# Masks written by VectorE instead of added by matmuls, and squares summed by TensorE, in a 16-head mixer and a stick-breaking layer

## The chip, the core and the metric

The program runs on one core of a Trainium2 chip. The metric is the device time of one execution in microseconds (us), the median over several runs. Engines are called PE (TensorE, with PEld for its weight loads), DVE (VectorE), ACT (ScalarE), POOL (GpSimd) and SP (SyncE, which issues most transfers).

## The reference

The input is one sequence of 256 tokens of width 1024, in float32. A first block with a mixer and a feed-forward part is followed by a second one with two layers: retention, and stick-breaking attention, each between feed-forward parts. What matters here are the two places with a mask and one with a sum of squares.

```python
# first block: differential attention (8 heads, two score maps each) and latent attention (8 heads)
def chunk_causal_attention(q, k, v, scale):
    ...
        q_chunk = (i * Q_BLOCK + jnp.arange(Q_BLOCK)) // CHUNK      # Q_BLOCK 128, CHUNK 64
        mask = key_chunk[None, :] <= q_chunk[:, None]
        sc = jnp.einsum('bhqd,bhkd->bhqk', qi, k, ...) * scale
        sc = jnp.where(mask, sc, jnp.float32(-1e30))
        p = jax.nn.softmax(sc, axis=-1).astype(v.dtype)
    ...
    oa = o1 - lam.astype(o1.dtype) * o2
    oa = rms_norm(oa, da_subln[l]) * (1.0 - lambda_init)
    ...
    cq = rms_norm(cq, q_a_norm[l])       # latents of 384 and 256 columns
    ckv = rms_norm(ckv, kv_a_norm[l])

# second block: strictly causal stick-breaking, 8 heads
        z = jnp.einsum('bhqd,bhkd->bhqk', q_blk, k) * scale
        mask = (kpos[None, :] < qpos[:, None])[None, None]
        log_one_minus = jnp.where(mask, jax.nn.log_sigmoid(-z), 0.0)
        rem = lax.cumsum(log_one_minus, axis=3, reverse=True) - log_one_minus
        a = jnp.where(mask, jnp.exp(jax.nn.log_sigmoid(z) + rem), 0.0)
```

With a chunk of 64 tokens and blocks of 128 queries, the first 64 queries of each block must not see the last 64 keys of that block. Only these two 64x64 corners of a head's scores are masked.

## The kernel before, in words

**Matmuls.** Activations lie with features on the partitions. Each float32 operand is split in a rounded part and a rest (`_hi`, `_lo`), and a product is made of three: hi by hi, hi by lo, lo by hi. The weights come in pieces by DMA into `w_raw` (3 buffers, issued by SP); ACT casts them to `w_hi` (L191), DVE subtracts to `w_lo` (L192), and each of the two has 12 buffers. `mm3` (L200) and `mat_steps` (L217) issue the matmuls: L200 with 128x512 or 128x256 columns, L217 with 128x256. Sums lie in PSUM: four banks for the projections (`ps`) and four for everything else (`S` scores, `pt` and `ot` transposes, `o` values, `c` sums, `ss` squares).

**Order.** The program is written once, in order, and a scheduler puts each instruction on its engine's queue by priority. Work of a head is raised in priority (`urgent`), and its matmuls are placed right behind the projection matmul that was written last before them (`at_pe`, which is `issue_after(self.behind)`). Between the steps of a head a `Filler` lets a set number of projection matmuls of later heads through: 30, 48 and 26 for the three steps of a differential head (`FILL_DA`), 8, 10 and 10 for a latent head (`FILL_MLA`), 10, 10 and 24 for a stick-breaking head, and 24 and 28 after the sums of squares of the two latents (`FILL_LATENTS`). So each head is a few short pieces on PE, each inside a stream of L200 and L217 matmuls.

**A head of the first mixer** (from some 55 to 245 us). `scores` (L665, L672) makes the scores S of 128 queries x 384 columns: 128 keys for the first query block, 256 for the second. A differential head (DA) has two of them, from 64-row products (rows 0 to 63 and 64 to 127 of the array); a latent head (MLA) has one, from a 128-row product (`k,q`) and a 64-row one (`kr,qr`). Ahead of these a one-row product of `masks` (L665) puts a large negative number in the two masked corners and zero elsewhere, and opens the sum. `softmax` takes maxima on DVE (L682), scales them (L684), exponentiates on ACT (L690) and takes reciprocals (L694). The probabilities are scaled on DVE (L896 in an MLA head), transposed one step later on PE (`pt`, L703), copied by ACT into `pts`, and multiplied with the values (L713, L714 in an MLA head, L840 in a DA head). A DA head's output is normalized (`oo`, L850) and transposed again (`ot`, L857) in the piece where the next head's scores begin.

**Sums of squares** (`sumsq`, L289 to L294). ACT squares the tiles of a latent (three of `cq`, two of `ckv`, each 128 x 256), POOL adds them up in `acc` (L291), and two fp32 matmuls of 128x1 (L294) sum over the partitions, one for each half of the tokens.

**A head of the stick-breaking layer** (from some 1305 to 1380 us). `scores` makes S (L1195), ACT and DVE form `zs` = S x scale (L1199) and the logarithms L, which are split in `lhi` and `llo`. `sums` makes the sums over later keys by products with a triangle and with ones (L1214 to L1217, L1219, L1220) and adds the mask with products of `neg_r` by a unit matrix (L1218, L1221). DVE adds `c` to `zs` and ACT exponentiates. The constants come in one tile, `ks`, by a transfer that POOL issues as the layer begins; its parts are rounded on DVE (`tri_r`, `neg_r`, `ones_r`, `ident_r`, a helper at L562).

Of the kernel before, what the change touches and what calls it, by code (L numbers as in the profile page):

```python
# [10 lines left out]
F32 = mybir.dt.float32  # L11
# [7 lines left out]
P = 128  # L19
T = 256  # L20
# [45 lines left out]
K_TRI, K_M01, K_NEG, NKS = 0, 128, 256, 384  # L66


def constants():
# [4 lines left out]
    m = np.zeros((1, 4 * P), np.float32)  # L74
    m[0, :P] = i < 64
    for at in (192, 448):
        m[0, at : at + 64] = NEG
# [6 lines left out]
    t[:, K_NEG : K_NEG + P] = np.where(i[:, None] >= i[None, :], NEG, 0.0)  # L84
# [10 lines left out]
    return c, t, d, m  # L95
# [52 lines left out]
class Build:  # L148
# [132 lines left out]
    def sumsq(self, n, tile):  # L281

        nc = self.nc
        ss = self.psa.tile([P, 2], F32, name="ss", tag="a")
        acc = self.tmp.tile([P, T], F32, name="acc", tag="acc", bufs=1)
        for i in range(n):
            src = tile(i)
            sq = acc if i == 0 else self.tmp.tile([P, T], F32, name="sq", tag="sq")
            nc.scalar.activation(sq, src, AF.Square)  # L289
            if i:  # L290
                nc.gpsimd.tensor_add(acc, acc, sq)  # L291
            yield i, src
        for b in range(2):
            nc.tensor.matmul(  # L294
                ss[:, b : b + 1], acc[:, b * P : (b + 1) * P], self.ones[:, 0:1],
                start=b == 0, stop=b == 1, skip_group_check=True,
            )
        self.ss = ss
# [242 lines left out]
    def setup_scores(self):  # L541
        nc, const, aps = self.nc, self.const, self.aps
        mk = self.tmp.tile([1, 4 * P], F32, name="mk", tag="sq")
        nc.gpsimd.dma_start(mk, aps["mk"])
        masks = self.rounded(const, "masks", mk)
        self.q0, self.k1 = masks[:, 0:P], masks[:, P:]

        lt = self.lam
        pr = self.tmp.tile([P, 2, 64], F32, name="pr", tag="a")
        l4 = lt.rearrange("p (a b) -> p a b", a=4)  # L550
        nc.vector.tensor_mul(pr, l4[:, 0:2, :], l4[:, 2:4, :])
        sm = self.sm.tile([P, 2], F32, name="lsum", tag="v")
        nc.vector.tensor_reduce(sm, pr, axis=AX.X, op=ALU.add)
        le = self.sm.tile([P, 2], F32, name="lexp", tag="v")
        nc.scalar.activation(le, sm, AF.Exp)
        self.nlam = const.tile([P, 1], F32, name="nlam")
        nc.vector.tensor_sub(self.nlam, le[:, 1:2], le[:, 0:1])
        nc.vector.tensor_scalar_add(self.nlam, self.nlam, -LAMBDA_INIT)
# [100 lines left out]
    def scores(self, Ss, parts):  # L659
# [3 lines left out]
        with self.at_pe():  # L663
            for S in Ss:
                mm(S, self.q0, self.k1, start=True, stop=False, skip_group_check=True)  # L665
            for b in range(2):
                at = slice(0, P) if b == 0 else slice(P, 3 * P)
                qs, ks = slice(b * P, (b + 1) * P), slice(0, (b + 1) * P)
                for n in range(len(parts[0])):
                    for S, qk in zip(Ss, parts):  # L670
                        q, k = qk[n]
                        mm(S[:, at], q[:, qs], k[:, ks], start=False, stop=n == len(parts[0]) - 1, skip_group_check=True)  # L672

    def softmax(self, Ss, scale):
# [5 lines left out]
        for e, S in enumerate(Ss):  # L680
            for b in range(2):
# [473 lines left out]
    def stick(self, X, R, before, row):  # L1155
        nc, tc = self.nc, self.tc
        spec = lambda c0: ("sb_w_in_2", (0,), range(c0, c0 + P))
        with tc.tile_pool(name="stick", bufs=1) as sp:
# [4 lines left out]
            neg_r = self.rounded(sp, "neg_r", ks[:, K_NEG : K_NEG + P])  # L1163
            ones_r = self.rounded(sp, "ones_r", self.ones)
            ident_r = self.rounded(sp, "ident_r", self.ident)
            m01 = ks[:, K_M01 : K_M01 + P]
# [22 lines left out]
            def scores(h):  # L1189
# [9 lines left out]
                nc.vector.tensor_scalar_mul(zs, S, SB_SCALE)  # L1199
# [9 lines left out]
            def sums(h):  # L1209
# [3 lines left out]
                with self.at_pe():  # L1213
# [3 lines left out]
                    mm(c[:, P : 2 * P], ones_r, llo[:, 2 * P :], start=False, stop=False)  # L1217
                    mm(c[:, 0:P], ident_r, neg_r, start=False, stop=True)  # L1218
                    mm(c[:, 2 * P :], tri_r, lhi[:, 2 * P :], start=True, stop=False)  # L1219
                    mm(c[:, 2 * P :], tri_r, llo[:, 2 * P :], start=False, stop=False)  # L1220
                    mm(c[:, 2 * P :], ident_r, neg_r, start=False, stop=True)  # L1221
# [177 lines left out]
```

## Time and profile before

| what | value |
|---|---|
| median of 3 runs | 1623.23 us (1621.54 to 1623.61) |
| profiled execution, time | 1622.01 us |
| its span | 1620.2 us |
| its mean granted PE clock | 0.997 |
| weights and the rest read from HBM | 284.65 MB, 176 GB/s over the span |

A span is the stretch between the first and the last instruction of the profiled execution. In a row of the timeline stand the start, the time of the group in us, engine, line, operation, the tiles written and read, the rows and columns of the weights, the shape of what streams, and the number of instructions taken together; in brackets the idle time before it and what ended it. A matmul of two fp32 operands runs as two passes and is counted as two instructions. Ends of matmuls are modelled and overlap, so starts are compared with starts.

### The profile page before, as it was taken

To read this page: it belongs to the slowest core of one execution; us is meant where nothing else is said; L and a number is where in the kernel's file an instruction comes from. 1 tells how busy PE (TensorE), PEld (TensorE's weight loads), DVE (VectorE), ACT (ScalarE), POOL (GpSimd) and SP (SyncE) were. 2 spreads that over 40 slices of the span, in tenths; PEclk is the share of its full clock that TensorE was granted. 3 is DMA by queue.
4 is the path that set the end of the run, shared out by engine and by line. 5 is a ranking of instruction groups with operands and counts; after the bars stand their busy time and mean duration, and the time that the engine had idled before them with its cause. 6 is when DMAs were issued, how large, how long until landed. Compare 5 with 4: busy or idle time off the path is not lost.

```text
span 1620.2 us, 22387 instructions
## 1 busy us (share of the span) xinstructions
PE 1606.6 (99%) x8258; PEld 1349.5 (83%) x8258; DVE 1061.3 (66%) x1948; ACT 904.0 (56%) x1792; POOL 90.1 (6%) x101
## 2 busy tenths in 40 slices
PE   9999999999999999999999999999999999999997
PEld 9898778888888888898888888878888899888886
DVE  7987656755556555777766565576655677666546
ACT  7655544755455554645546555475554656655545
POOL 1100000200002000100000000030000200000002
PEclk9999999999999999999999999999999999999999
DMA  7535435555545555455455555555555453555451
GB/s 254 211 122 180 161 104 195 195 182 186 184 175 208 187 177 195 168 187 178 164 190 178 188 180 193 190 195 182 182 182 182 172 191 134 178 182 182 182 184 64
DMA packets 46862, 288.60 MB, mean 178 GB/s; under 512 B 5968, under 2 KB 9168, under 8 KB 13856
## 3 DMA queue, kind: packets, MB, share of 16 engines
q1 hardware_dynamic: 44240, 279.29, 48.7%
q0 software_dynamic: 2080, 7.67, 1.4%
q8 instruction: 65, 1.06, 0.3%
q14 instruction: 45, 0.37, 0.1%
q10 hardware_dynamic: 432, 0.20, 0.0%
HBM read 284.65 MB, written 1.05 MB: 176 GB/s over the span
## 4 chain that ended last, share of the span: by engine, by line
PE 95%; DVE 2%; DMA 1%; issue 1%; ACT 1%; SPq 0%; POOL 0%; POOLq 0%; DVEq 0%; ACTq 0%
PE ps L200 78%; PE ps L217 9%; PE at L638 1%; PE S L672 1%; PE xt L435 1%; DMA w_raw<-in_w 1%; DVE w_lo L192 1%; PE o L200 1%; PE o L713 0%; PE S L665 0%; PE S L1079 0%; PE S L1195 0%; DMA h<-in_x 0%; PE pt L703 0%; PE o L840 0%
## 5 line engine op out<-in xcount | busy, mean ns | idle before, releaser
L192 DVE TENSOR_TENSOR w_lo<-w_raw,w_hi 128x512 fp32r<-128x512 f32 x1054 | 707.5, 687 | 363.9 <-ACT w_hi L191 360.2
L191 ACT CAST w_hi<-w_raw 128x512 fp32r<-128x512 f32 x1054 | 638.7, 621 | 482.7 <-PE ps L200 355.3
L200 PE MATMUL ps<-w_hi,x_hi 128*128 128x512 f32 (+1 forms) x1280 | 489.4, 382 | 1.1 <-ACT x_hi L439 1.1
L200 PE MATMUL ps<-w_hi,x_lo 128*128 128x512 f32 (+1 forms) x1280 | 483.5, 378 | 1.2 <-DVE x_lo L441 1.2
L200 PE MATMUL ps<-w_lo,x_hi 128*128 128x512 f32 (+1 forms) x1280 | 482.4, 377 | 0.0
L200 PEld LDWEIGHTS ps<-w_hi,x_lo 128*128 128x128 f32 x1280 | 241.1, 188 | 47.3 <-DVE x_lo L441 2.4
L200 PEld LDWEIGHTS ps<-w_hi,x_hi 128*128 128x128 f32 x1280 | 241.3, 188 | 43.9 <-ACT x_hi L439 1.5
L200 PEld LDWEIGHTS ps<-w_lo,x_hi 128*128 128x128 f32 x1280 | 241.4, 189 | 42.0
L200 PE MATMUL ps<-w_hi,a_hi 128*128 128x512 f32 x440 | 176.8, 402 | 0.0
L200 PE MATMUL ps<-w_hi,a_lo 128*128 128x512 f32 x440 | 173.4, 394 | 0.0
L200 PE MATMUL ps<-w_lo,a_hi 128*128 128x512 f32 x440 | 172.6, 392 | 0.0
L302 POOL TENSOR_TENSOR r<-v,mhalf 128x1 f32<-128x1 f32 (+1 forms) x50 | 63.7, 1274 | 1239.8 <-DVE v L390 1100.6
L217 PE MATMUL ps<-x_hi,w_hi 128*128 128x256 f32 x440 | 114.7, 289 | 0.2 <-DVE h L780 0.2
L217 PE MATMUL ps<-x_hi,w_lo 128*128 128x256 f32 x440 | 112.5, 284 | 0.0
L200 PEld LDWEIGHTS ps<-w_hi,a_lo 128*128 128x128 f32 x440 | 82.6, 188 | 21.4
L200 PEld LDWEIGHTS ps<-w_lo,a_hi 128*128 128x128 f32 x440 | 82.7, 188 | 19.1
L200 PEld LDWEIGHTS ps<-w_hi,a_hi 128*128 128x128 f32 x440 | 82.7, 188 | 18.3
L217 PEld LDWEIGHTS ps<-x_hi,w_hi 128*128 128x128 f32 x440 | 84.1, 191 | 1.3 <-issue 0.7
L217 PEld LDWEIGHTS ps<-x_hi,w_lo 128*128 128x128 f32 x440 | 84.2, 192 | 0.6 <-DVE w_lo L192 0.3
L217 PE MATMUL ps<-x_lo,w_hi 128*128 128x256 f32 x440 | 77.5, 283 | 0.0
L633 DVE SCALAR_TENSOR_TENSOR a<-ps,R,s 128x512 f32<-128x512 f32 (+1 forms) x60 | 42.2, 703 | 52.2 <-PE ps L200 44.6
L274 ACT CAST a_hi<-at 128x512 fp32r<-128x512 f32 (+1 forms) x60 | 33.1, 552 | 67.9 <-PE at L638 67.9
(282 smaller groups left out, 1506.1 us busy)
## 6 DMA issues: line engine op xcount, KB each, us to landing
w_raw<-in_w SPq DMA_DIRECT2D x256, 1024.0 KB, 4.8
gr<-in_rows POOLq DMA_DIRECT2D x10, 512.0 KB, 4.6
w_raw<-in_w SPq DMA_DIRECT2D x12, 256.0 KB, 4.9
w_raw<-in_w SPq DMA_DIRECT2D x6, 384.0 KB, 3.2
w_raw<-in_w SPq DMA_DIRECT2D x3, 512.0 KB, 3.6
h<-in_x SPq DMA_DIRECT2D x4, 256.0 KB, 4.9
h<-in_x POOLq DMA_DIRECT2D x1, 1024.0 KB, 7.9
out<-h SPq DMA_DIRECT2D x3, 256.0 KB, 2.5
```

What stands on the lines that cost most here:

```text
L191: nc.scalar.copy(hi[:, :m], r[:, c0:c1])
L192: nc.vector.tensor_sub(lo[:, :m], r[:, c0:c1], hi[:, :m].bitcast(F32))
L200: mm = lambda a, b, **k: nc.tensor.matmul(ps, a, b, skip_group_check=True, **k)
L217: mm = lambda *a, **k: self.nc.tensor.matmul(*a, skip_group_check=True, **k)
L274: nc.scalar.copy(hi, src)
L302: self.nc.gpsimd.tensor_tensor(r, v, self.mhalf[:, :n], op=ALU.pow)
L435: nc.tensor.transpose(pt[:, i, :], self.h[:, b, k * P : (k + 1) * P], self.ident)
L633: nc.vector.scalar_tensor_tensor(a, banks[1], R[:, b : b + 1], s, op0=ALU.mult, op1=ALU.mult)
L638: nc.tensor.transpose(pt[:, i, :], a[:, i * P : (i + 1) * P], self.ident)
L672: mm(S[:, at], q[:, qs], k[:, ks], start=False, stop=n == len(parts[0]) - 1, skip_group_check=True)
```

## The change

Three things change.

1. `scores` issues no mask product; the first product of each query block opens its sum. A new function `masked` writes the negative number with a DVE memset into the two corners of S (partitions 0 to 63, columns 64 to 127 and 320 to 383), ahead of the maxima: 24 memsets, two in a DA head and one in an MLA head. The `mk` constants, their transfer and their rounding cast go.
2. In stick-breaking the mask is added as S is scaled (`scalar_tensor_tensor` for `tensor_scalar_mul`), with a mask tile of 384 columns. The 16 products with `neg_r` go, as do the casts of `neg_r` and `ident_r`; `ks` has 640 columns for 384.
3. `sumsq` keeps the squares of all tiles (`sqs`), and PE adds them: 10 matmuls of 128x1 in place of 4, and no additions on POOL (3 before).

```diff
-K_TRI, K_M01, K_NEG, NKS = 0, 128, 256, 384
+K_TRI, K_M01, K_NEG, NKS = 0, 128, 256, 640
...
-    t[:, K_NEG : K_NEG + P] = np.where(i[:, None] >= i[None, :], NEG, 0.0)
+    for at in (K_NEG, K_NEG + 2 * P):
+        t[:, at : at + P] = np.where(i[:, None] >= i[None, :], NEG, 0.0)
...
-        acc = self.tmp.tile([P, T], F32, name="acc", tag="acc", bufs=1)
+        sq = self.tmp.tile([P, 3, T], F32, name="sqs", tag="acc", bufs=1)
         for i in range(n):
             src = tile(i)
-            sq = acc if i == 0 else self.tmp.tile([P, T], F32, name="sq", tag="sq")
-            nc.scalar.activation(sq, src, AF.Square)
-            if i:
-                nc.gpsimd.tensor_add(acc, acc, sq)
+            nc.scalar.activation(sq[:, i, :], src, AF.Square)
             yield i, src
-        for b in range(2):
-            nc.tensor.matmul(
-                ss[:, b : b + 1], acc[:, b * P : (b + 1) * P], self.ones[:, 0:1],
-                start=b == 0, stop=b == 1, skip_group_check=True,
-            )
+        for i in range(n):
+            for b in range(2):
+                nc.tensor.matmul(
+                    ss[:, b : b + 1], sq[:, i, b * P : (b + 1) * P], self.ones[:, 0:1],
+                    start=i == b == 0, stop=i == n - 1, skip_group_check=True,
+                )
...
-            for S in Ss:
-                mm(S, self.q0, self.k1, start=True, stop=False, skip_group_check=True)
             for b in range(2):
...
-                        mm(S[:, at], q[:, qs], k[:, ks], start=False, stop=n == len(parts[0]) - 1, skip_group_check=True)
+                        mm(S[:, at], q[:, qs], k[:, ks], start=n == 0, stop=n == len(parts[0]) - 1, skip_group_check=True)
+
+    def masked(self, S):
+
+        tail = S.rearrange("p (c n) -> p c n", n=64)
+        self.nc.vector.memset(tail[0:64, 1:6:4, :], NEG)
...
         for e, S in enumerate(Ss):
+            self.masked(S)
             for b in range(2):
...
-            neg_r = self.rounded(sp, "neg_r", ks[:, K_NEG : K_NEG + P])
             ones_r = self.rounded(sp, "ones_r", self.ones)
-            ident_r = self.rounded(sp, "ident_r", self.ident)
-            m01 = ks[:, K_M01 : K_M01 + P]
+            m01, neg = ks[:, K_M01 : K_M01 + P], ks[:, K_NEG : K_NEG + 3 * P]
...
-                nc.vector.tensor_scalar_mul(zs, S, SB_SCALE)
+                nc.vector.scalar_tensor_tensor(zs, S, SB_SCALE, neg, op0=ALU.mult, op1=ALU.add)
...
-                    mm(c[:, 0:P], ident_r, neg_r, start=False, stop=True)
...
-                    mm(c[:, 2 * P :], ident_r, neg_r, start=False, stop=True)
```

The change also moves what stays. Names in the rows below: `ot` is the transposed output of the head before, S the scores, `x_hi`, `x_lo`, `cq_`, `ckv_` the projections' activations. The queue of PE at a DA head whose scores stand between the two transposes of the head before; before the change:

```order
L217 MATMUL ps<-x_lo,w_hi 128x256 x2
L857 MATMUL ot<-kc,oo 128x128
L665 MATMUL S<-masks 128x384
L857 MATMUL ot<-kc,oo 128x128
L665 MATMUL S<-masks 128x384
L672 MATMUL S<-k,q 128x128 x2
L672 MATMUL S<-k,q 128x256 x2
L217 MATMUL ps<-x_hi,w_hi 128x256
```

and after it (the two S of a head are not told apart by name; a row stands for the tile of one half of the rows):

```order
L214 MATMUL ps<-x_lo,w_hi 128x256 x4
L852 MATMUL ot<-kc,oo 128x128
L661 MATMUL S<-k,q 128x128
L852 MATMUL ot<-kc,oo 128x128
L661 MATMUL S<-k,q 128x128
L661 MATMUL S<-k,q 128x256 x2
L214 MATMUL ps<-x_hi,w_hi 128x256
```

The place of each mask is taken by a score product of 128 columns.

The queue of PE where the last DA head's output is transposed and a latent head's scores begin, before the change:

```order
L217 MATMUL ps<-ckv_h,w_hi 128x256
L217 MATMUL ps<-ckv_h,w_lo 128x256
L217 MATMUL ps<-ckv_h,w_hi 128x256
L217 MATMUL ps<-ckv_h,w_lo 128x256
L857 MATMUL ot<-kc,oo 128x128
L665 MATMUL S<-masks 128x384
L672 MATMUL S<-k,q 128x128
L857 MATMUL ot<-kc,oo 128x128
L672 MATMUL S<-kr,qr 128x128
L672 MATMUL S<-k,q 128x256
L672 MATMUL S<-kr,qr 128x256
```

and after it:

```order
L214 MATMUL ps<-cq_l,w_hi 128x256 x2
L214 MATMUL ps<-ckv_h,w_hi 128x256
L852 MATMUL ot<-kc,oo 128x128
L661 MATMUL S<-k,q 128x128
L661 MATMUL S<-kr,qr 128x128
L852 MATMUL ot<-kc,oo 128x128
L661 MATMUL S<-k,q 128x256
L661 MATMUL S<-kr,qr 128x256
L698 MATMUL pt<-kc,p 128x128 x3
```

The piece begins three projection matmuls earlier, behind one of the latent's projection matmuls instead of four.

The queue of DVE in an MLA head, before the change (`w_lo` and `ob_lo` are low halves, `mx`, `nm`, `rs`, `p` the softmax):

```order
L192 TENSOR_TENSOR w_lo<-w_raw,w_hi 128x512 x2
L275 TENSOR_TENSOR ob_lo<-o,ob_hi 128x256
L192 TENSOR_TENSOR w_lo<-w_raw,w_hi 128x512
L682 TENSOR_REDUCE mx<-S 128x1 x2
L684 TENSOR_SCALAR nm<-mx 128x2
L694 RECIPROCAL rs<-sums 128x2
L896 TENSOR_SCALAR p<-p,rs 128x128
L896 TENSOR_SCALAR p<-p,rs 128x256
```

and after it:

```order
L189 TENSOR_TENSOR w_lo<-w_raw,w_hi 128x512 x2
L272 TENSOR_TENSOR ob_lo<-o,ob_hi 128x256
L189 TENSOR_TENSOR w_lo<-w_raw,w_hi 128x512
L666 MEMSET S 64x2x64
L677 TENSOR_REDUCE mx<-S 128x1 x2
L679 TENSOR_SCALAR nm<-mx 128x2
L689 RECIPROCAL rs<-sums 128x2
L891 TENSOR_SCALAR p<-p,rs 128x128
L891 TENSOR_SCALAR p<-p,rs 128x256
```

The memset stands between the weights' subtraction and the maxima, which read what it writes; nothing else has moved.

More of the change, by code (lines that the diff above doesn't have):

```diff
@@ L73, in constants @@
     c[:, K_ID : K_ID + P] = np.eye(P)
[L74 to L77, printed above, removed]
     base = (np.float64(10000.0) ** (np.arange(32) * (2 / 64))).astype(np.float32)
@@ L94, in constants @@
         d[:, at + P : at + 2 * P] = zeta[:, None] * xi[None, :] / 16.0
-    return c, t, d, m
+    return c, t, d
 class Weights:
@@ L541, in setup_scores @@
     def setup_scores(self):
[L542 to L546, printed above, removed]
+        nc, const = self.nc, self.const
         lt = self.lam
@@ L1216, in sums @@
                     mm(c[:, P : 2 * P], ones_r, lhi[:, 2 * P :], start=False, stop=False)
-                    mm(c[:, P : 2 * P], ones_r, llo[:, 2 * P :], start=False, stop=False)
-                    mm(c[:, 0:P], ident_r, neg_r, start=False, stop=True)
+                    mm(c[:, P : 2 * P], ones_r, llo[:, 2 * P :], start=False, stop=True)
                     mm(c[:, 2 * P :], tri_r, lhi[:, 2 * P :], start=True, stop=False)
-                    mm(c[:, 2 * P :], tri_r, llo[:, 2 * P :], start=False, stop=False)
-                    mm(c[:, 2 * P :], ident_r, neg_r, start=False, stop=True)
+                    mm(c[:, 2 * P :], tri_r, llo[:, 2 * P :], start=False, stop=True)
                 nc.vector.tensor_add(zs, zs, c)
@@ L1382 @@
         "pos2": inputs["positions_2"],
-        **dict(zip(("kc", "ks", "kd", "mk"), constants())),
+        **dict(zip(("kc", "ks", "kd"), constants())),
     }
```

## Prediction

> **What bounds the kernel now.** I read the page's busy totals first, then its chain of work that ended last, then busy time by stage, and last the timeline of PE at each place that the change touches.
>
> ```profile
> PE 1606.6 (99%) x8258; PEld 1349.5 (83%) x8258; DVE 1061.3 (66%) x1948; ACT 904.0 (56%) x1792; POOL 90.1 (6%) x101
> ```
> ```profile
> PE 95%; DVE 2%; DMA 1%; issue 1%; ACT 1%; SPq 0%; POOL 0%; POOLq 0%; DVEq 0%; ACTq 0%
> ```
>
> PE is busy in 99% of the span and holds 95% of the chain, so whatever leaves PE's stream shortens the span, as long as the other engines still deliver in time. Whether they do is asked stage by stage. The busy time by window (length, then PE, weight load, DVE, ACT, POOL, clock, DMA share, GB/s) for the first mixer's four parts and for the stick-breaking layer:
>
> ```profile
> 30.00:60.00 30.00, 29.77 (x202) 27.03 (x202) 28.55 (x64) 18.30 (x38) 8.78 (x6) 1.00 0.69 254
> 60.00:80.00 20.00, 20.00 (x118) 16.61 (x118) 19.70 (x51) 14.69 (x37) 0.69 (x1) 1.00 0.38 123
> 80.00:180.00 100.00, 99.84 (x629) 85.24 (x628) 76.38 (x182) 56.73 (x149) 4.51 (x6) 1.00 0.43 147
> 180.00:260.00 80.00, 79.50 (x383) 59.80 (x384) 48.14 (x112) 39.19 (x97) 1.30 (x2) 1.00 0.39 140
> 1318.00:1376.00 58.00, 57.55 (x430) 54.86 (x429) 47.54 (x99) 38.59 (x75) 0.00 (x0) 1.00 0.36 128
> ```
>
> PE has no hole anywhere here: it idles 0.23 us in the first window and nothing in the second. DVE is nearly as full as PE up to 80 us (28.55 of 30, 19.70 of 20) and has a quarter to two fifths of its time free after that. So from 80 us on DVE can take new work, and before that it is the engine to fear.
>
> **The change part by part.** *DA heads, masks back to back (2 heads).* The change takes out the two masks of a head (L665); the first product of scores then opens the sum by itself.
>
> ```profile
> 62.17 0.61 PE L665 MATMUL S<-masks 1*128 1x384 f32 x2
> 62.71 0.93 PE L672 MATMUL S<-k,q 64*128 64x128 f32 x8
> ```
>
> Two masks hold PE from 62.17 to 62.71, 0.54 us. The scores' weight load changes the number of active rows either way (128 to 1 before, 128 to 64 after), so I expect them where the first mask stands now: 2 x -0.54 = -1.09.
>
> *DA heads, masks between the transposes of the head before (6 heads).*
>
> ```profile
> 78.52 0.27 PE L857 MATMUL ot<-kc,oo 128*128 128x128 f32 x1
> 78.72 0.43 PE L665 MATMUL S<-masks 1*128 1x384 f32 x1
> 79.09 0.33 PE L857 MATMUL ot<-kc,oo 128*128 128x128 f32 x1
> 79.35 0.44 PE L665 MATMUL S<-masks 1*128 1x384 f32 x1
> 79.72 0.93 PE L672 MATMUL S<-k,q 64*128 64x128 f32 x8
> 80.57 0.39 PE L217 MATMUL ps<-x_hi,w_hi 128*128 128x256 f32 x1
> ```
>
> Each mask takes 0.37 (78.72 to 79.09, 79.35 to 79.72), the whole piece 2.05. Afterwards a score product of one half of the rows slips into each mask's place, and only the 256-column ones still run as a pair on the two row halves. A 64-row product that stands alone takes 0.41 (207.29 to 207.70, the MLA rows below). The piece becomes 0.20 (transpose) + 0.41 + 0.26 (transpose) + at most the 0.85 that all eight passes take now = 1.72: -0.33 per head, 6 x -0.33 = -1.98. Ends: the slipped-in product costs nothing beyond what it saves in the pair (it takes some 0.2 of the 0.85): -0.55 per head; or the halves no longer pair at all, the 0.85 doubling: 1.72 + 0.85 = 2.57, +0.52 per head. I take the first since the order still alternates the halves.
>
> *MLA heads (8).* What a product with 128 rows costs next to others with 128 rows, and what the same form costs next to a mask:
>
> ```profile
> 204.36 0.59 PE L713 MATMUL o<-pts,vb 128*128 128x256 f32 x2
> 204.79 0.38 PE L714 MATMUL o<-pts,vb 128*128 128x128 f32 x2
> 204.94 0.48 PE L200 MATMUL ps<-w_hi,oa_h 128*128 128x512 f32 x1
> ```
> ```profile
> 205.95 0.40 PE L200 MATMUL ps<-w_lo,oa_h 128*128 128x512 f32 x1
> 206.19 0.39 PE L200 MATMUL ps<-w_hi,oa_l 128*128 128x512 f32 x1
> 206.51 0.43 PE L665 MATMUL S<-masks 1*128 1x384 f32 x1
> 206.87 0.49 PE L672 MATMUL S<-k,q 128*128 128x128 f32 x2
> 207.29 0.48 PE L672 MATMUL S<-kr,qr 64*128 64x128 f32 x2
> 207.70 0.70 PE L672 MATMUL S<-k,q 128*128 128x256 f32 x2
> ```
>
> Among equals, two passes of 128x128 take 0.15 (204.79 to 204.94), their loads hidden; beside a change in row count the same form takes 0.42 (206.87 to 207.29), and an L200 that is followed by the mask takes 0.32 where its neighbour takes 0.24. So the exposed load is what a mask brings, on both of its sides. After the change the first k,q follows an L200 with 128 rows, thus at 206.19 + 0.24 = 206.43 in place of 206.87: -0.44. Its two passes then need 0.15 and one change to 64 rows, for which a transpose before a mask gives the size (0.26 from 79.09 to 79.35 for one pass of about 0.1): 0.15 + 0.16 = 0.31 in place of 0.42, -0.11 more. Sum -0.55, times 8 = -4.4. Ends: the second part does not come (-0.44 each, -3.5); the first load stays exposed too, and only the mask's own 0.36 goes (-2.9).
>
> The Trainium skill, "TensorE: Matmul & The Clock Gate", in Part 3 under "The mechanism", states that a weight load overlaps running products only when its row group differs. By that rule this first load would stay exposed, -2.9 in place of -4.4; the rows at 204.36 to 204.94, equal rows with loads hidden, do not agree with it.
>
> *Stick-breaking (16 products), latents (+6 products), and a wait.* The first row's product with neg_r goes; the fp32 128x1 sums of squares come; the last pair is the one place in the mixer where PE waits for the head's output.
>
> ```profile
> 1338.78 0.27 PE L1218 MATMUL c<-neg_r,ident_r 128*128 128x128 f32 x1
> 1338.88 0.28 PE L1219 MATMUL c<-lhi,tri_r 128*128 128x128 f32 x1
> ```
> ```profile
> 47.02 0.50 PE L294 MATMUL ss<-ones,acc 128*128 128x1 f32 x4
> 47.38 0.36 PE L217 MATMUL ps<-x_hi,w_hi 128*128 128x256 f32 x1
> ```
> ```profile
> 191.38 0.28 PE L217 MATMUL ps<-ckv_h,w_lo 128*128 128x256 f32 x1
> 192.17 0.30 PE L857 MATMUL ot<-kc,oo 128*128 128x128 f32 x1 [0.51 <-DVE oo L850]
> ```
>
> A masking product costs 0.10 to 0.11: 16 x -0.11 = -1.8, all on PE among equals. Of the squares, two products make four passes (x4) in 0.36, 0.09 each; by the 0.11 of the masking products, to be safe, 6 more products of 2 passes cost 12 x 0.11 = +1.3 (+1.1 by the 0.09). The three POOL additions that they replace free nothing: in this window PE runs without a hole to fill. At 191.38 the next product comes 0.79 later where 0.12 is usual; the order now puts that transpose three L217 earlier, so PE reaches it 3 x 0.12 sooner and waits that much longer: +0.36.
>
> *DVE.* 24 memsets of 64x2x64 are new. Groups by form (busy, mean ns):
>
> ```profile
> L520 DVE MEMSET ones<- x1: 165/165/165, 0.8 to 0.8; 128x128 f32 x1
> ```
> ```profile
> L682 DVE TENSOR_REDUCE mx<-S 128x1 f32<-128x128 f32 x24 | 6.8, 285 | 7.5 <-PE S L672 7.5
> ```
> ```profile
> L1199 DVE TENSOR_SCALAR zs<-S 128x384 f32<-128x384 f32 x8 | 4.4, 552 | 0.4 <-ACT u L1197 0.4
> ```
> ```profile
> L633 DVE SCALAR_TENSOR_TENSOR a<-ps,R,s 128x512 f32<-128x512 f32 x50 | 37.4, 747 | 47.7 <-PE ps L200 40.2 <-issue 3.8 <-ACT s L632 3.8
> ```
>
> A memset of 128 columns took 165 ns into SBUF and a reduction of 128 columns out of PSUM 285: between 24 x 0.165 = 4.0 and 24 x 0.285 = 6.8 us of DVE. I cost it at nothing for PE: the probabilities it delays are used a whole head later, with 28 filler products between, and only the 60 to 80 us window lacks room, where w_lo runs ahead of use. If that cover is gone, the price is in the rivals. Queued behind the memset are the next w_lo subtractions; PE waits for those. The zs edit is 552 ns for 384 columns (1.44 per column) against 747 for 512 (1.46) for the other form: nothing. Four rounding casts fewer is DVE time that nobody waits for.
>
> *The constants' transfer.* ks grows from 192 to 320 KB, on POOL's queue.
>
> ```profile
> ks<-in_ks POOLq DMA_DIRECT2D x1, 192.0 KB, 4.4
> ```
> ```profile
> h<-in_x POOLq DMA_DIRECT2D x1, 1024.0 KB, 7.9
> ```
> ```profile
> 1287.48 0.23 DVE L562 CAST tri_r<-ks 128x128 fp32r<-128x128 f32 x1 [0.85 <-DMA ks<-in_ks]
> ```
> ```profile
> 1289.25 0.41 PE L200 MATMUL ps<-w_hi,x_lo 128*128 128x512 f32 x1
> ```
>
> DVE already waits 0.85 for it, at the head of a layer, and the activations' low halves (for PE at 1289.25) are queued behind the cast. A size in between should land at 4.4 to 7.9; the extra, 0 to 3.5, is set off by two casts less (2 x 0.23). I take nothing, being nearest the 192 KB row; at the upper end 3.0 us are lost.
>
> *Sum:* -1.1 - 2.0 - 4.4 - 1.8 + 1.3 + 0.4 = -7.6. The profiled execution took 1622.0 (span 1620.2); it lies 1.2 below the median of the runs shown, 1623.2. Against the median: 1623.2 - 7.6 = 1615.6; I say 1615.5.
>
> **The rivals.** *The first load stays exposed in the MLA heads*: -2.9 in place of -4.4, 1617.0. For it: every row at a mask shows an exposed load. Against it: the 204.36 rows. The Trainium skill's sentence above is the rule that speaks for it.
>
> *The pairing of the DA row halves is lost*: +0.52 instead of -0.33 on six heads, +5.1, 1620.6. For it: the transposes separate the two first products. Against it: two passes of a 64-row product alone take 0.41, and the eight as they stand 0.85, so half of the pair already runs alone cheaply.
>
> *DVE gives it back.* Up to 80 us DVE is the fuller engine. If w_lo is what sets the pace through the DA heads, PE's 3.1 us there turn into waits and 16 memsets x 0.165 to 0.285 = 2.6 to 4.6 are added: -7.6 + 3.1 + 2.6 to 4.6 = -1.9 to +0.1, 1621.3 to 1623.3, no change that can be told. For it: 19.70 of 20. Against it: PE idles nothing in that window, so w_lo is early there, and from 80 to 180 DVE is free for 23.6 us.
>
> *Slower.* The same, with a dearer memset: no row shows a memset into PSUM. Slower begins where 16 of them cost 4.5 + 3.25 = 7.75, at 0.49 us each, 1.7 times a reduction of the same columns from PSUM: from 1626.5 up.
>
> **How the numbers follow.** The measurement tells 0.2%, 3.25 us, from no change: 1620.0 to 1626.5 is the same. Forecast 0.61, exposed load 0.12, a further gain below 0.05, pairing lost 0.08, DVE gives back 0.09, slower 0.05. The first three are faster, 0.78; the next two the same, 0.17; slower 0.05. A clock row adds to both ends:
>
> ```profile
> 1092.00:1096.00 4.00, 3.32 (x13) 2.83 (x13) 3.60 (x12) 2.75 (x10) 0.54 (x1) 0.57 0.36 152
> ```
>
> The granted clock was 0.57 in these 4 us, some 1.3 us of PE time, which an earlier stream may lose or meet again elsewhere. The forecast's own range is 1613.3 to 1617.5. Down, the best ends of the DA heads (6 x 0.22 = 1.3), the clock (1.3) and no longer wait at 191 (0.4) give 1612.5, with the runs' spread 1612.0. Up, it takes in the lost pairing and the beginning of DVE's case: 1621.0. That leaves out some 1.5 in 10.
>
> **What would show it.** Right: PE's busy time about 7 us less and DVE's about 4 to 6 more; the piece of a DA head with transposes 1.7 long in place of 2.05; in an MLA head the last L200, k,q and kr 0.24 and 0.3 apart; no w_lo wait on PE between 30 and 180; the wait at the first MLA head near 0.9; a memset of 0.17 to 0.29. Wrong: PE waits for w_lo or p in the first mixer, or for x_lo at 1289; a k,q 0.3 after its L200; score products with long gaps between; or PE's stream shorter while the chain passes to DVE.

## The result, and the profile after

| kernel | median us | runs | ratio to before, 95% interval |
|---|---|---|---|
| before | 1622.63 (1621.54 to 1623.61) | 4 | |
| changed | 1615.76 (1613.31 to 1617.02) | 4 | 0.995 [0.9937, 0.9962] |

The forecast was 1615.5, with 1612.0 to 1621.0 around it. The profiled execution of the changed kernel took 1613.31 us, its span 1611.5. Its busy totals and the chain that ended last:

```profile
PE 1596.3 (99%) x8230; PEld 1344.3 (83%) x8230; DVE 1064.0 (66%) x1969; ACT 903.7 (56%) x1792; POOL 85.5 (5%) x97
```
```profile
PE 97%; DVE 1%; DMA 1%; ACT 1%; issue 1%; POOL 0%; SPq 0%; POOLq 0%; DVEq 0%; ACTq 0%
```

PE holds still more of the chain (97% for 95%). Lines are 3 to 8 lower in the changed file: L200 is now L197, L217 L214, L294 L289, L672 L661, L857 L852.

Both programs issue the same 7320 projection matmuls (L200 and L217 before) in nearly the same order, so the start of number n in one timeline less that in the other tells how far the one is ahead at that point. The stretches between some of them, in us:

| stretch (projection matmul number) | before | changed | |
|---|---|---|---|
| 1 to 264, start of the kernel | 39.54 | 39.88 | +0.34 |
| to 301, the latents' squares | 5.62 | 6.77 | +1.15 |
| to 1151, the heads of the first mixer | 201.35 | 194.39 | -6.96 |
| to 4901, feed-forward, retention | 823.74 | 823.75 | +0.01 |
| to 5001, between two layers | 29.46 | 28.40 | -1.06 |
| to 5901 | 200.62 | 200.61 | -0.01 |
| to 6401, stick-breaking | 96.88 | 95.04 | -1.84 |
| to 7301, the rest | 202.72 | 202.72 | 0.00 |

The time left at the three places that were changed and nowhere else, but for 1.06 us in a stretch that the change doesn't touch. That is the clock: the row of 1092 to 1096 us showed 0.57 before (in the trace, 0.50 for 3.4 us of these four), and there is no such stretch now.

```profile
1090.00:1100.00 10.00, 10.00 (x46) 8.29 (x45) 9.37 (x22) 7.06 (x16) 3.62 (x4) 1.00 0.49 161
```

So the change itself gave 6.96 - 1.15 + 1.84 = 7.65 us, and the other 1.06 of the profile's 8.7 were chance (shown by e10 below). The timeline of PE at the pieces of the prediction, first a DA head with transposes, then an MLA head:

```profile
78.56 0.27 PE L852 MATMUL ot<-kc,oo 128*128 128x128 f32 x1
78.76 0.49 PE L661 MATMUL S<-k,q 64*128 64x128 f32 x2
79.18 0.33 PE L852 MATMUL ot<-kc,oo 128*128 128x128 f32 x1
79.43 0.92 PE L661 MATMUL S<-k,q 64*128 64x128 f32 x6
80.28 0.38 PE L214 MATMUL ps<-x_hi,w_hi 128*128 128x256 f32 x1
```
```profile
195.70 0.40 PE L197 MATMUL ps<-w_hi,oa_l 128*128 128x512 f32 x1
195.94 0.38 PE L661 MATMUL S<-k,q 128*128 128x128 f32 x2
196.25 0.48 PE L661 MATMUL S<-kr,qr 64*128 64x128 f32 x2
196.67 0.70 PE L661 MATMUL S<-k,q 128*128 128x256 f32 x2
```

The first piece takes 1.72 us (78.56 to 80.28), 2.05 before. In the second, k,q starts 0.24 after the L197 ahead of it, as one L197 after another, and kr 0.31 later: the loads of equal rows are hidden. The weight loads (PEld) show it themselves, first before the change, then after it:

```profile
206.51 0.18 PEld L665 LDWEIGHTS S<-masks 1*128 1x128 f32 x1 [0.36 <-issue]
206.87 0.30 PEld L672 LDWEIGHTS S<-k,q 128*128 128x128 f32 x2 [0.18 <-issue]
```
```profile
195.70 0.43 PEld L661 LDWEIGHTS S<-k,q 128*128 128x128 f32 x2
196.25 0.29 PEld L661 LDWEIGHTS S<-kr,qr 64*128 64x128 f32 x2
```

Where the number of rows changes (the mask, k,q behind the mask, kr behind k,q), the load starts only when its own product does. Between equal rows it starts with the product ahead: the first load of k,q at 195.70, together with the L197, 0.24 before its own product. Why it can't start earlier at a change of rows is not shown. The squares, the waits of the first two MLA heads for the DA heads' outputs, and the three groups of DVE that were in question:

```profile
46.98 1.39 PE L289 MATMUL ss<-ones,sqs 128*128 128x1 f32 x12
48.24 0.36 PE L214 MATMUL ps<-x_hi,w_hi 128*128 128x256 f32 x1
```
```profile
177.39 0.33 PE L852 MATMUL ot<-kc,oo 128*128 128x128 f32 x1 [0.23 <-DVE oo L845]
```
```profile
189.76 0.30 PE L852 MATMUL ot<-kc,oo 128*128 128x128 f32 x1 [0.87 <-DVE oo L845]
```
```profile
L666 DVE MEMSET S<- x24: 165/165/165, 58.3 to 235.4; 64x128 f32 x24
```
```profile
L1192 DVE SCALAR_TENSOR_TENSOR zs<-S,ks x8: 548/552/558, 1313.4 to 1361.0; 128x384 f32<-128x384 f32 x8
```
```profile
1280.85 0.23 DVE L553 CAST tri_r<-ks 128x128 fp32r<-128x128 f32 x1 [1.13 <-DMA ks<-in_ks]
```

Twelve passes of the first latent take 1.26 where four took 0.36. The wait at the second of these heads grew from 0.51 to 0.87, the one at the first is new. A memset into PSUM costs what one into SBUF did, 0.165. The wait for the longer constants is 1.13, it was 0.85 before. By windows, as before the change:

```profile
60.00:80.00 20.00, 20.00 (x123) 17.05 (x121) 19.69 (x53) 15.31 (x38) 0.69 (x1) 1.00 0.38 132
80.00:180.00 100.00, 99.77 (x623) 85.81 (x621) 82.00 (x203) 59.39 (x154) 5.12 (x6) 1.00 0.46 150
```

DVE is as full as it was up to 80 us, and PE still has no hole there; from 80 to 180 DVE has 18 us free.

### The profile page after: what moved, and what is told of

The parts are those of the page before. It is cut to its first block, busy times and chain, and to the rows that moved or that the text cites. A ratio compares the mean times of both kernels' runs of the same rounds, so it can differ in the third digit from the quotient of the medians.

```text
span 1611.5 us, 22352 instructions
## 1 busy us (share of the span) xinstructions
PE 1596.3 (99%) x8230; PEld 1344.3 (83%) x8230; DVE 1064.0 (66%) x1969; ACT 903.7 (56%) x1792; POOL 85.5 (5%) x97
## 4 chain that ended last, share of the span: by engine, by line
PE 97%; DVE 1%; DMA 1%; ACT 1%; issue 1%; POOL 0%; SPq 0%; POOLq 0%; DVEq 0%; ACTq 0%
PE ps L197 79%; PE ps L214 10%; PE S L661 2%; PE at L629 1%; PE xt L430 1%; DMA w_raw<-in_w 1%; PE o L197 1%; PE o L708 0%; PE S L1074 0%; PE S L1188 0%; PE pt L698 0%; PE o L835 0%; ACT w_hi L188 0%; DVE w_lo L189 0%; PE ot L1111 0%
## 5 line engine op out<-in xcount | busy, mean ns | idle before, releaser
L197 PE MATMUL ps<-w_hi,x_hi 128*128 128x512 f32 (+1 forms) x1280 | 489.1, 382 | 1.1 <-ACT x_hi L434 1.1
L197 PE MATMUL ps<-w_hi,x_lo 128*128 128x512 f32 (+1 forms) x1280 | 483.0, 377 | 1.2 <-DVE x_lo L436 1.2
L197 PE MATMUL ps<-w_lo,x_hi 128*128 128x512 f32 (+1 forms) x1280 | 482.2, 377 | 0.0
L197 PEld LDWEIGHTS ps<-w_hi,x_lo 128*128 128x128 f32 x1280 | 240.9, 188 | 47.2 <-DVE x_lo L436 2.4
L197 PEld LDWEIGHTS ps<-w_hi,x_hi 128*128 128x128 f32 x1280 | 241.1, 188 | 44.0 <-ACT x_hi L434 1.5
L197 PEld LDWEIGHTS ps<-w_lo,x_hi 128*128 128x128 f32 x1280 | 241.4, 189 | 42.0
L197 PE MATMUL ps<-w_hi,a_hi 128*128 128x512 f32 x440 | 176.8, 402 | 0.0
L197 PE MATMUL ps<-w_hi,a_lo 128*128 128x512 f32 x440 | 173.4, 394 | 0.0
L197 PE MATMUL ps<-w_lo,a_hi 128*128 128x512 f32 x440 | 172.6, 392 | 0.0
L214 PE MATMUL ps<-x_hi,w_hi 128*128 128x256 f32 x440 | 114.7, 289 | 1.1 <-ACT w_hi L188 0.7
L214 PE MATMUL ps<-x_hi,w_lo 128*128 128x256 f32 x440 | 112.3, 284 | 0.2 <-DVE w_lo L189 0.2
L197 PEld LDWEIGHTS ps<-w_hi,a_lo 128*128 128x128 f32 x440 | 82.6, 188 | 21.4
L197 PEld LDWEIGHTS ps<-w_lo,a_hi 128*128 128x128 f32 x440 | 82.7, 188 | 19.0
L197 PEld LDWEIGHTS ps<-w_hi,a_hi 128*128 128x128 f32 x440 | 82.6, 188 | 18.4
L214 PEld LDWEIGHTS ps<-x_hi,w_hi 128*128 128x128 f32 x440 | 84.0, 191 | 2.5 <-ACT w_hi L188 0.9
L214 PEld LDWEIGHTS ps<-x_hi,w_lo 128*128 128x128 f32 x440 | 84.2, 192 | 0.8 <-DVE w_lo L189 0.4
L214 PE MATMUL ps<-x_lo,w_hi 128*128 128x256 f32 x440 | 77.4, 283 | 0.0
```

Source lines behind the costliest of these rows:

```text
L197: mm = lambda a, b, **k: nc.tensor.matmul(ps, a, b, skip_group_check=True, **k)
L214: mm = lambda *a, **k: self.nc.tensor.matmul(*a, skip_group_check=True, **k)
```

## The experiments

The theory is that PE is the bound, that each piece returns what its products and their exposed weight loads (those that no product hides) took, and that DVE hides the memsets. The rivals are that DVE gives the gain back, that only the masks' own time returned, and that the pairs of row halves and the hidden loads are something else than the prediction took them for. Stretches below are those of the table, each from the experiment's own timeline; medians are compared within their own session, where before had 1623.12 (e1 to e4), 1622.76 (e5 to e8) and 1623.53 (e9 to e11).

### Each part undone

**e1, the DA masks on PE again** (their constants, transfer and cast come back too)

```diff
+            pe = len(Ss) == 2
+            for S in Ss if pe else ():
+                mm(S, self.q0, self.k1, start=True, stop=False, skip_group_check=True)
...
-                        mm(S[:, at], ..., start=n == 0, ...)
+                        mm(S[:, at], ..., start=n == 0 and not pe, ...)
...
-            self.masked(S)
+            if not (len(Ss) == 2):
+                self.masked(S)
```

> The changed kernel with one part undone: the masks of the 8 differential heads are products on PE again (16 of them), the latent heads keep their memsets. Theory (PE is the bound, what leaves its stream comes back one for one): the first mixer loses what these heads gave, 2 x 0.54 + 6 x 0.33 = 3.1 us, so 1615.8 + 3.1 = 1618.9, and between the same two projection products at the mixer's two ends the time is 3.1 longer than in the changed kernel, with all of it at the eight pieces of scores. Rival (up to 80 us DVE sets the pace, and the memsets cost there what PE gave): no loss, 1615.8 or up to 2.6 less, since 16 memsets of 0.165 leave DVE.

Measured: 1618.64 us (1616.78 to 1619.93), ratio 0.9973 [0.9963, 0.9983]. The heads' stretch took 197.30, 2.91 more than in the changed kernel, and the piece at 80 us is again 2.05 long. At the eight pieces themselves 3.05 was lost; 0.26 more went at 133 us (see "What no term names" below), and 0.43 came back at the first MLA head, where the changed kernel waits 0.23 for `oo` and this one does not. The theory holds; DVE had nothing to give back.

**e2, the MLA masks on PE again** (the same edit, with `len(Ss) == 1`)

> The changed kernel with the masks of the 8 latent heads as products on PE again, the differential heads keep their memsets. Theory: each of these heads gave 0.55 us, 0.36 for the mask itself and 0.20 for weight loads that stood exposed beside the change from 128 rows to 1 and back; 8 x 0.55 = 4.4, so 1620.2. Rival (only the mask's own 0.36 came back, the rest is another place's): 2.9, so 1618.7.

Measured: 1621.65 us (1618.91 to 1623.86), ratio 0.999 [0.9981, 0.9999], more than either expected. The heads' stretch took 199.75, 5.36 more. The six plain pieces are 0.55 or 0.56 longer each. The first MLA head lost 0.17 and the second 1.97, and at the second the clock fell:

```profile
192.00:196.00 4.00, 4.00 (x17) 3.16 (x16) 1.89 (x5) 1.30 (x5) 0.00 (x0) 0.63 0.72 262
```

In the trace the granted clock is 0.50 from 193.1 to 196.5. That costs up to 3.4 x 0.5 = 1.7 us, and by the stretch between two layers (below) such a fall costs 1.0 to 1.2; without it the masks cost 3.7 to 4.4, which is the theory's figure and not the rival's 2.9. The plain pieces decide it by themselves: 0.56 each and not 0.36. The median lies high because other runs of this kernel seem to have met the low clock too: the five runs of 1618.91 to 1620.45 us have a mean granted clock of 0.998 or 0.999, the six of 1621.65 to 1623.86 one of 0.996 or 0.997. Only one run has a trace, so where it fell in the others is not known.

**e3, the stick-breaking part undone**

```diff
-                nc.vector.scalar_tensor_tensor(zs, S, SB_SCALE, neg, op0=ALU.mult, op1=ALU.add)
+                nc.vector.tensor_scalar_mul(zs, S, SB_SCALE)
...
+                    mm(c[:, 0:P], ident_r, neg_r, start=False, stop=True)
...
+                    mm(c[:, 2 * P :], ident_r, neg_r, start=False, stop=True)
```

> The changed kernel with the stick-breaking part undone (16 masking products, the casts, the short constants' tile). Theory: 16 x 0.11 = 1.8 us, all of it within the layer, so 1617.6; the layer's head, where the constants land, takes the same time with 192 KB as with 320. Rival (the longer transfer costs at the layer's head what the products gave): less than 1 us apart, and the part of the layer ahead of the first score products is shorter by that than in the changed kernel.

Measured: 1616.34 us (1615.58 to 1618.66), ratio 0.9964 [0.9951, 0.9976]. The layer's stretch took 96.91, 1.87 more; the one ahead of it, with the constants' transfer, 200.65 for 200.61. The cast of the triangle waited 0.88 for 192 KB and 1.13 for 320:

```profile
1281.02 0.23 DVE L552 CAST tri_r<-ks 128x128 fp32r<-128x128 f32 x1 [0.88 <-DMA ks<-in_ks]
```

The 0.25 more is about what the two casts that went away had taken (0.27 from start to start). The theory holds in the trace; the medians of this part alone (0.6 apart from the first four runs of the changed kernel) would not have told it from nothing.

**e4, the squares added on POOL again** (the lines of `sumsq` as before the change)

> The changed kernel with the squares of the latents added by POOL again, 4 products of 128x1 in place of 10. Theory: the six products cost PE 1.2 us (0.90 at 47 us, 0.26 at 51) and nothing waits for the latents, so 1614.6, a gain over the changed kernel. Rival (the earlier latents are worth what the products cost, since rq is wanted by later work): no gain, 1615.8 or more, with a wait of PE or DVE for POOL behind 50 us.

Measured: 1614.91 us (1614.15 to 1615.23), ratio 0.9951 [0.9938, 0.9963], not to be told from the changed kernel. The latents' stretch took 6.81, no shorter than 6.77. The six products were gone, but now PE waited for POOL:

```profile
50.18 2.67 POOL L288 TENSOR_TENSOR acc<-acc,sq 128x256 f32<-128x256 f32 x1 [13.18 <-ACT acc L286]
```
```profile
52.90 0.61 PE L291 MATMUL ss<-ones,acc 128*128 128x1 f32 x4 [1.11 <-POOL acc L288]
```

The wait that the rival named is there, though not for its reason: the sum itself comes late. In the kernel before, PE reached these products at 50.42 and POOL's addition was done at 50.36, 0.06 us ahead. In this run it came 1.11 too late. The addition stands at the edge: taking it off POOL cost PE 1.15 us and, by these two traces, saves a wait of 0 to 1.1.

### How much DVE can hide

**e5, four memsets for one**

```diff
-        self.nc.vector.memset(tail[0:64, 1:6:4, :], NEG)
+        for _ in range(4):
+            self.nc.vector.memset(tail[0:64, 1:6:4, :], NEG)
```

> The changed kernel with each memset of a masked corner written four times in a row (96 in place of 24, the extra 72 do nothing new): 72 x 0.165 = 11.9 us more of DVE, 7.9 of it in the differential heads. This also makes the scheduler keep the two transposes of a head's output together ahead of the next scores, the same order on PE as in e8, so it is compared with e8. Theory (DVE hides behind PE's work): within 0.5 us of e8, PE without waits for w_lo. Rival (DVE is the pace up to 80 us): up to 7.9 us longer than e8, with waits of PE for w_lo or for the probabilities.

Measured: 1614.26 us (1612.43 to 1615.77), ratio 0.9946 [0.9934, 0.9957]. The order was not the one the expectation names: the timeline has the first score product between the transposes, as the changed kernel has.

```profile
79.81 0.27 PE L853 MATMUL ot<-kc,oo 128*128 128x128 f32 x1
80.01 0.48 PE L661 MATMUL S<-k,q 64*128 64x128 f32 x2
```

So it is compared with the changed kernel, with some pieces a few projection products elsewhere. The heads' stretch took 193.42, 0.97 less, with 11.9 us more of DVE. So DVE hides at least 11.9 us beside the 4.0 that the change gave it; why the stretch is shorter was not tried.

**e6, ten memsets, and e11, seven** (the same edit)

> As e5, with ten memsets each (240): 216 x 0.165 = 35.6 us more of DVE, 23.8 in the differential heads, 3.0 per head of that kind and 1.5 per latent head. PE's order is that of e8 and e5. Theory: DVE had 25 us free between 30 and 180, so it is about filled; the head's chain (maxima wait 3 us longer) is still covered by 28 to 48 projection products, so between 0 and 6 us longer than e8, the loss between 60 and 110. Rival (DVE sets the pace): 20 us or more.

> The changed kernel with each memset of a masked corner written seven times (144 more, 144 x 0.165 = 23.8 us of DVE, 2.0 per differential head and 1.0 per latent head). It lies between e5 (11.9 us more of DVE, nothing lost) and e6 (35.6 more, 20 lost in the mixer). Theory (DVE has slack, and past it each us of DVE is a us of the kernel): the loss begins between the two; by a straight line through e6, 35.6 - 20 = 15.6 us of slack, 23.8 - 15.6 = 8 us lost. Rival (what broke in e6 is a threshold, the weights' transfers queued behind the copies of late rope halves): nearly nothing lost, under 2 us.

Measured: e6 1636.3 us (1632.84 to 1642.29), ratio 1.0085 [1.007, 1.01]; e11 1628.19 (1624.72 to 1630.88), 1.0028 [1.0019, 1.0038]. The heads' stretches took 214.52 and 204.73, 20.1 and 10.3 more than in the changed kernel. The order on PE differs in some places here too (not that of e8, as e6's expectation has it). The first row is e6, the second e11:

```profile
80.00:120.00 40.00, 32.24 (x204) 28.72 (x203) 34.10 (x110) 11.12 (x35) 1.86 (x2) 0.83 0.28 80
```
```profile
80.00:120.00 40.00, 36.44 (x285) 33.64 (x283) 35.64 (x105) 16.32 (x47) 1.48 (x2) 1.00 0.42 147
```

In these 40 us PE idles 7.8 and 3.6 us where the changed kernel had no hole, and in e6 ACT, which casts the weights, is busy for 11.1 us there, in the changed kernel for 24.5. In e6 (from 30 to 180 us) its casts waited 28.9 us for weights, 18.3 in the changed kernel; and scores waited for a copy on SP's queue, which also carries the weights:

```profile
ACT w_hi L188 <- DMA w_raw<-in_w: 28.9, 9, 7.3
```
```profile
84.15 1.62 PE L661 MATMUL S<-k,q 64*128 64x128 f32 x4 [0.71 <-DMA k<-x]
```

The theory's 0 to 6 us for e6 was wrong. The rival's 20 came out, but a DVE that sets the pace would be full where PE idles, and it is not. It is busy for 34.10 and 35.64 of these 40 us, and from 60 to 80 us for 15.43 and 16.42 of 20, where the changed kernel has 19.69. The rows point to SP's queue, where weights stand behind the copies of `q` and `k`, which wait for DVE. In the changed kernel (first rows) a piece of weights goes out right behind the copies of `q`; in e11 (second rows) none goes out from 60 to 83 us:

```profile
67.74 2.42 SPq L607 DMA_DIRECT2D q<-x  x4
70.25 0.53 SPq L176 DMA_DIRECT2D w_raw<-in_w  x1
```
```profile
73.72 2.42 SPq L607 DMA_DIRECT2D q<-x  x4
80.51 2.41 SPq L607 DMA_DIRECT2D k<-x  x4
83.03 8.15 SPq L176 DMA_DIRECT2D w_raw<-in_w  x3
```

In e6 the clock adds to the loss: the first row above shows 0.83. In the trace it is 0.50 for 17.0 us of the heads' stretch in three pieces, the first of them here; in e11 and in the changed kernel it never falls there.

```profile
84.10:90.90 6.80, 6.75 (x23) 5.26 (x24) 5.15 (x25) 0.78 (x2) 0.00 (x0) 0.50 0.53 169
```

PE was busy for 15.2 of the 17.0, so up to 7.6 of e6's 20.1 us are the clock. PE's idle time in the heads' stretch tells more: 1.1 us in the changed kernel, 0.7 in e5, 8.5 in e11, 12.0 in e6. For 11.9 us of DVE each it grew by 7.8 from e5 to e11 and by 3.5 from e11 to e6, which looks more like a step past e5 than like a straight line. The line's 8 came near e11's 10.3 by luck, since the 20 it was drawn through holds the clock; the rival's step was put too late (under 2 at e11). That the late copies start the loss is argued from these rows and not shown: no run puts them on another queue.

### The order of the scores' products

**e7, in a latent head both 128-row products first**

```diff
-            for b in range(2):
-                at = slice(0, P) if b == 0 else slice(P, 3 * P)
-                qs, ks = ...
-                for n in range(len(parts[0])):
+            for n in range(len(parts[0])):
+                for b in range(2):
+                    at = slice(0, P) if b == 0 else slice(P, 3 * P)
+                    qs, ks = ...
...
-                        mm(S[:, at], ..., start=n == 0, ...)
+                        mm(S[:, at], ..., start=n == 0 and (b == 0 or len(Ss) == 2), ...)
```

> The changed kernel with the four products of a latent head's scores in another order: both of k,q (128 rows), then both of kr,qr (64 rows), in place of taking turns. The products are the same; the number of active rows changes twice per head in place of four times. Theory (a change in rows keeps a weight load from being hidden, 0.16 to 0.2 us each): 2 x 8 changes less, -2.6 to -3.2 us against the changed kernel, 1612.6 to 1613.2; the score piece takes 0.3 to 0.4 less. Rival (loads hide only where the rows differ): longer than the changed kernel.

Measured: 1612.33 us (1609.87 to 1613.11), ratio 0.9933 [0.9921, 0.9945]; the heads' stretch 191.51, 2.88 less. The piece of an MLA head:

```profile
197.59 0.40 PE L197 MATMUL ps<-w_hi,oa_l 128*128 128x512 f32 x1
197.82 0.82 PE L661 MATMUL S<-k,q 128*128 128x128 f32 x4
198.57 0.92 PE L661 MATMUL S<-kr,qr 64*128 64x128 f32 x4
199.42 0.51 PE L197 MATMUL ps<-w_hi,oa_h 128*128 128x512 f32 x1
```

From the first score product to the next projection it takes 1.60 us, where the changed kernel takes 1.98 (195.94 to 197.92): (1.98 - 1.60) / 2 = 0.19 for each change of rows that is saved, the products being the same. The theory holds, and the rival had it the wrong way round.

**e8, a DA head's scores behind both transposes**

```diff
                 for b in range(2):
-                    nc.tensor.transpose(pt[:, b * P : (b + 1) * P], oo[:, b, :], self.ident)
+                    last = nc.tensor.transpose(pt[:, b * P : (b + 1) * P], oo[:, b, :], self.ident).ins
+            self.behind = last
```

> The changed kernel with the scores of a differential head placed behind both transposes of the output of the head before, in place of between them (the placing mark of the scores is the second transpose). The products are the same. Theory (a score product of 64 rows that stands alone between two transposes pays two changes of rows and runs without its partner of the other half): the piece takes 1.2 in place of 1.73 us, six pieces, -3 us, 1612.8. Rival (the pair of halves does not matter, only the number of products): the same as the changed kernel, 1615.8.

Measured: 1612.41 us (1611.34 to 1613.17), ratio 0.9934 [0.9922, 0.9946]; the heads' stretch 192.48, 1.91 less. The piece takes 1.16 (79.65 to 80.81), as the theory has it, and each of the six gave 0.56; but further on PE waited for a PSUM bank that DVE had not yet read:

```profile
79.65 0.38 PE L852 MATMUL ot<-kc,oo 128*128 128x128 f32 x2
79.96 0.93 PE L661 MATMUL S<-k,q 64*128 64x128 f32 x8
80.81 0.39 PE L214 MATMUL ps<-x_hi,w_hi 128*128 128x256 f32 x1
```
```profile
166.37 0.36 PE L214 MATMUL ps<-ckv_h,w_hi 128*128 128x256 f32 x1 [1.06 <-DVE t L597]
```

6 x 0.56 = 3.4, and this wait took most of the difference to the 1.9 that were measured.

**e9, both orders** (the edits of e7 and e8 together)

> The changed kernel with both new orders: scores of a differential head behind both transposes (as e8), and both 128-row products of a latent head ahead of both 64-row ones (as e7). Theory: the two gains lie at different pieces and add. Between the same projection products at the mixer's ends the changed kernel takes 194.4 us, e7 191.5, e8 192.5 (it lost 1.2 of its gain to a wait for a PSUM bank that DVE frees): 194.4 - 2.9 - 1.9 = 189.6, and the run 4.8 below the changed kernel beside it. Rival (the shorter pieces bring the next wait for DVE into the open): less than 3.5 gained, with a longer wait for oo or for the bank.

Measured: 1609.84 us (1609.02 to 1611.12), ratio 0.9917 [0.9903, 0.993]; the heads' stretch 188.92, 5.5 less than in the changed kernel's first profile (4.8 expected) and 5.2 less than in e10's. The two gains add: the limit of the rival (3.5) is passed, and PE's waits for DVE in this stretch are 1.8 us together, 2.3 in e8. It beats both kernels: 13.7 us below before and 5.0 below the changed kernel in the same session (e10). Its busy totals:

```profile
PE 1591.4 (99%) x8230; PEld 1342.3 (84%) x8230; DVE 1063.4 (66%) x1969; ACT 903.0 (56%) x1792; POOL 85.0 (5%) x97
```

As many instructions as the changed kernel, and 4.9 us less of PE.

**e10, the changed kernel again**

> The changed kernel, unaltered, once more beside the others. Theory: the stretch from the first mixer's latents to the last projection repeats within 0.2 us; the profiled time differs by what the first 47 us take, which were 39.5 to 42.1 long in the ten profiles so far, and by 1.0 if a stretch of lower clock occurs. Median 1615.8, between 1614.5 and 1616.5. Rival (the earlier four runs were lucky): above 1617.

Measured: 1614.86 us (1614.18 to 1615.78), ratio 0.9948 [0.9935, 0.996]. The profiled run took 1615.5 us, 2.2 more than the first one, and the table says where: 41.15 for 39.88 in the start, and 29.62 for 28.40 between the two layers, where the clock was low this time (0.50 from 1088.4 to 1091.8, across the two rows):

```profile
1080.00:1090.00 10.00, 7.27 (x32) 5.03 (x31) 9.15 (x19) 8.95 (x25) 1.47 (x2) 0.92 0.32 105
1090.00:1100.00 10.00, 10.00 (x45) 8.48 (x44) 8.53 (x23) 7.13 (x18) 1.98 (x4) 0.91 0.30 105
```

The heads' stretch was 194.07 for 194.39, a little more apart than the 0.2 expected, so differences of 0.3 between two profiles of it tell nothing; the stretch of stick-breaking 95.03 for 95.04. So the low clock after the pause between two layers comes and goes with the same kernel, and the 1.06 us of the first comparison belong to no part of the change.

## Why the prediction was right

- *DA heads, back to back*: -1.09 forecast. The projection behind these pieces moved ahead by 0.55 and 0.54. All eight DA pieces together gave 3.05 when e1 undid them, 3.07 forecast.
- *DA heads with transposes*: 1.72 forecast for the piece and 1.72 measured; each of the six steps is 0.32 or 0.33. The last six passes take the 0.85 that all eight took, the upper end of "at most". The pairing is not quite as assumed: the first short product stands alone, but the second starts together with the first 256-column one (79.43 and 79.44 in the trace), so the halves still run in pairs there. e8, with both short products behind the transposes, is worth another 0.56.
- *MLA heads*: -0.55 each forecast. Six of them gave 0.55 or 0.56. The first two have a transpose inside; between the projections on both sides of them they gave 0.05 and 0.24. Waits for oo of 0.23 and 0.87 stand where 0 and 0.51 stood, +0.59 against the +0.36 of the prediction, which saw the second wait grow and not the first one come: PE reached it earlier by what the DA heads had given, and with the DA masks back, in e1, that wait is gone. So the eight heads gave 3.64 for 4.4 - 0.36 = 4.04, the term of the mixer that was mis-sized.
- *What no term names*: 0.45 came at a place without a mask. Before the change (row below) PE waited there for DVE, and now it doesn't; e1 takes 0.26 of it back and e2 nothing, so it goes with the DA heads. Some 0.2 was lost again near 224 us, where the products for `o` now stand one projection product later.

```profile
134.29 0.51 PE L200 MATMUL ps<-w_hi,ckv_h 128*128 128x512 f32 x1 [0.16 <-DVE q L885]
```

- *The first load stays exposed*: no. It follows an L197 by 0.24 at 195.94. The Trainium skill, "TensorE: Matmul & The Clock Gate", Part 3, "The mechanism", has loads overlapped only with products of other row groups; here they are hidden between equal rows, and e7, with fewer changes of rows, gained 2.88. The measurement decides against that sentence for such products.
- *Latents*: +1.3 forecast, +1.15 measured, nearer to the lower end (+1.1) that the four passes of before gave. That POOL's additions "free nothing" was right for that trace by 0.06 us only; e4 shows the wait of 1.11 that they can bring.
- *Stick-breaking*: -1.8 forecast, -1.84 measured, and 1.87 by e3. The zs form costs 552 ns as before; the wait for the longer transfer is 0.28 longer, and the two missing casts paid for it, with 0.27 and not the 2 x 0.23 of the prediction, since casts start 0.14 apart.
- *DVE*: the memset came out at the lower bound, 0.165, so 24 of them cost 4.0 us; but DVE's busy time rose by only 2.7 and not by the 4 to 6 that the prediction named as a sign, since three casts are gone (it counted four, and left them out of that sign). That DVE gives it back was wrong by a wide margin (e5); that begins somewhere between four and seven times the memsets' time (e5, e11). "A quarter to two fifths" of free time holds for the mixer, in the stick-breaking row it is less (47.54 of 58 busy, 18% free). PE's busy time fell by 10.3 and not by about 7: the span is 8.7 shorter, and PE idles 1.6 more.
- *The sum*: -7.6 forecast, 6.96 - 1.15 + 1.84 = 7.65 measured between the same products. The mechanism was right in the main, but that the two agree to 0.1 is luck: 0.4 less from the MLA heads, 0.15 less for the latents and the 0.25 that no term names (0.45 - 0.2) cancel. Against the medians it reads 6.9 in the first session and 8.7 in e10's; the clock and the start of the kernel make up such differences, and the prediction's bound for the clock (1.3) covered its 1.06.

## What to carry to other kernels

When one engine is the bound, cost each small product by the start of its neighbours and not by its own length: here a mask that held PE for 0.36 us cost 0.56, the rest being weight loads that were no longer hidden where the number of active rows changes. Then look for other orders of the same products with fewer such changes; two of them gave 5.0 us, two thirds of what the change itself gave, with no work removed. And compare traces between the same instructions on both sides of a short piece: that told parts of 0.3 us from each other where medians of the whole run differ by 1 us from session to session. Look at the granted clock before a loss is put down to an engine: in e6 it was up to 7.6 of 20.1 us.

## What the runs showed of the hardware that was not expected

- In twelve of the thirteen profiles the first 264 projection products took between 39.5 and 42.1 us, and 42.9 in e11, with nearly the same code ahead of them, while the last stretch of the table took 202.70 to 202.74 in all of them. Much of the difference between profiles lies in this start, in which transfers are densest (0.77 of the DMA engines' time in the first 47 us of the changed kernel). Why it varies was not tried.
- Waits of PE are sometimes followed by a granted clock of 0.50 for 3.4 us, and sometimes not, with the same kernel: between the two layers PE waits three times within 5 us (0.5, 1.1 and 1.2 us) in the first profile of the changed kernel and in e10 alike, and the clock fell in e10 alone. A window that takes in more than the fall shows a mean (0.57, 0.63, 0.92 above). The stretch between the two layers took 29.4 to 29.6 us in the four of the thirteen profiles with such a fall there and 28.4 in the other nine, so a fall cost 1.0 to 1.2 us. In e2 the fall came some 3 us after a wait of 0.88 us, for oo at an MLA head.
